# A hybrid attention block: the gate rows of the forgetting heads by broadcast loads from DRAM, and the head norm in three VectorE steps

## The chip, the cores and the metric

The kernel runs on one core of one Trainium2 chip. The metric is the device time of one execution in microseconds, where lower is better. A core has five engines with instruction streams of their own, which wait for each other by semaphores: TensorE (PE; the loading of its stationary operand is listed as PEld), VectorE (DVE), ScalarE (ACT), GpSimd (POOL) and SyncE (SP), which in this kernel issues nearly all DMA transfers. On-chip memory is SBUF (128 partitions) and PSUM, into which TensorE accumulates.

## The reference, cut to what matters

One layer with 512 positions (`T`), a width of 2048, eight stick-breaking heads ("sb"), eight forgetting heads ("fox") of 128 columns each, and a feed-forward part of 8192.

```python
def head_rmsnorm(o, g):
    of = o * lax.rsqrt(jnp.mean(o * o, axis=-1, keepdims=True) + EPS)
    ...
    return of * g

def forgetting_attention(q, k, v, log_f):
    c = lax.cumsum(log_f, axis=2)
    ...
        z = einsum('bhqd,bhkd->bhqk', qb, kb) * scale
        z = z + c[:, :, q0:end, None] - c[:, :, None, :end]
        p = softmax(where(causal, z, -inf), axis=-1)
        outs.append(einsum('bhqk,bhkd->bhqd', p, vb))

def reference(...):
    h = rmsnorm(x, g_attn)
    [qa, ka, va, qf, kf, vf, f] = split(h @ w_in)
    log_f = log_sigmoid(f + b_f)
    mixed = concat(head_rmsnorm(stick_breaking_attention(qa, ka, va), g_out_sb),
                   head_rmsnorm(forgetting_attention(qf, kf, vf, log_f), g_out_fox))
    x = x + mixed @ w_out
    x = x + relu(rmsnorm(x, g_mlp) @ w_up) ** 2 @ w_down
    return rmsnorm(x, g_final)
```

All inputs and the output are float32. For the change two things matter: in a forgetting head the row `-c[k]` is added to every row of the scores, and each head's output is divided by its root mean square over the 128 columns.

## The kernel before

**Arithmetic.** TensorE works on a 32-bit form (`fp32r`) of less than full precision, so every operand is split into a high and a low half: ScalarE casts the high half (`split`, L71 and L74), VectorE subtracts it to get the low half (L72, L75), and `mm3` (L104 to L106) makes one product of three matmuls. The products with W_out, W_up and W_down use seven products of half-size blocks in place of eight, which needs sums of weight blocks beforehand.

**Stages.** From the start to about 58 us x is transposed and normalised (`prepare`, `transpose_x`), while the first V projection and the eight gate columns f are accumulated over the 16 chunks of 128 rows (`accumulate_v`). Until about 640 us a loop `for n in range(0, 2 * NH, 2)` runs over pairs of heads, the forgetting heads 6, 7, 0 to 5 first and then the stick-breaking ones. For each head `project_q` makes q and k (two loads of `w_in` in `load_w`, L94, each followed by casts `wh` and subtractions `wl`, and 48 matmuls `accq`), and `attend_fox` or `attend_sb` computes the head. `sums_of_weights` prepares W_out beside that: it loads 2 MB of it into `mixed`, splits and subtracts, and stores `wraws`, `whigh` and `wsums` to DRAM scratch. Then come W_out, W_up and W_down, up to the end.

**Order.** In the attention part nobody writes the order out by hand. The tile framework runs a simulated timeline over the program and merges the heads' work (`attend` runs inside `tc.high_priority()`) with the projections; each engine then gets one fixed order. The order depends on which buffers are free. W_up and W_down follow an order of their own. SP's queue is one stream in that order too: an instruction on SP that waits for a semaphore holds up every transfer behind it.

**The gate row.** After the first V projection the gates' logarithms are summed along the positions by matmuls with a triangle of ones (`cps`), giving `cq`, with positions on the partitions and one column for each head. `cq` is split into a rounded part (`cr`) and the remainder, both copied into the zeroed tile `chl`, transposed by four matmuls (`cT`, L425) and cast into `ckT` (L427), with the two parts of each head in rows h and 8 + h. A selection matrix `nsel` is built at the start with GpSimd (L389, L391) and VectorE (L393): for each head it has -1 in the rows h and 8 + h, for all 128 columns. In `attend_fox` a matmul of `nsel` with `ckT` (L306) gives the negative gate row on all 128 partitions in PSUM, and ScalarE copies it to `cb` in SBUF (L308). VectorE then adds it to the scores together with the query's gate (`w`, L312), GpSimd masks (L243), and the softmax follows (L317 maximum, L318, L320 Exp, L321, L323).

**The head norm.** `weigh` (L246 to L286) transposes the probabilities (`pt`, L251), splits them, multiplies with V into `o`, squares `o`, and sums the squares over the 128 columns by two matmuls with ones into `q`, named `ssq` in the profile (L282, L283). VectorE makes `va = q / P + EPS` (L284), ScalarE makes Ln and Exp (L110, L111), so `ra` is a first value of 1/sqrt(va), and three VectorE steps (L112 to L114) improve it by one Newton step, `ra * (1.5 - 0.5 * va * ra * ra)`. The last step multiplies with the head's gain `gv` (L286) into `mixed`. For the last head (`left == 0`) the sums lie in a half of the score buffer.

**Buffers.** In the attention part PSUM has one buffer with the tag "o" (`cps`, `cT`, `ck`, `o` and `ssq` take turns in it) and one with the tag "s" (scores, `pt`). `cb` has one buffer (tag "ul5"). The weights have three buffers each (`wraw`, `wh`, `wl`).

Of the kernel before, what the change touches and what calls it, by code (L numbers as in the profile page):

```python
# [8 lines left out]
F32 = mybir.dt.float32  # L9
F32R = mybir.dt.float32r  # L10
# [4 lines left out]
P = 128  # L15
# [20 lines left out]
def block_kernel(ctx, tc, x, g_attn, w_in, b_f, g_out_sb, g_out_fox, w_out, g_mlp, w_up, w_down, g_final, y):  # L36
# [71 lines left out]
    def rsqrt(out, v, a, b):  # L108

        act.activation(a, v, AF.Ln)  # L110
        act.activation(a, a, AF.Exp, scale=-0.5)  # L111
        dve.scalar_tensor_tensor(b, a, -0.5, v, op0=ALU.mult, op1=ALU.mult)  # L112
        dve.tensor_tensor(b, b, a, op=ALU.mult)
        dve.scalar_tensor_tensor(out, b, 1.5, a, op0=ALU.add, op1=ALU.mult)  # L114
# [28 lines left out]
    g_rest = cp.tile([P, KC + 2 * NH], F32, name="g_rest")  # L143
    g_up, g_sb, g_fx = g_rest[:, :KC], g_rest[:, KC:KC + NH], g_rest[:, KC + NH:]
    bf = cp.tile([P, NH], F32, name="bf")
    cp.tile([P, 16], F32, name="pad1")
    sums = cp.tile([P, TB, 4], F32, name="ss1")
    ss1, last_sum, before_last = sums[:, :, :2], sums[:, 0, 2:3], sums[:, 1, 2:3]
    ss2 = cp.tile([P, TB, 4], F32, name="ss2")
# [2 lines left out]


    wsums = dp.tile([P, NH // 2, 4, 2, 2, NT], F32, name="wsums")
    whigh = dp.tile([P, NH // 2, 2, NT], F32, name="whigh")

    wraws = [dp.tile([P, NH // 2, 2, 2, NT], F32, name=f"wraws{p}") for p in (1, 2)]
# [8 lines left out]
    with tc.tile_pool(name="att", bufs=1, side="right", reuse_waits="tile") as at:  # L166
# [59 lines left out]
        def wide(name, dt=F32):  # L226
            return at.tile([P, 1280], dt, tag=name, name=name)
# [18 lines left out]
        def weigh(h, v, hc, w, gv, left=2):  # L246

            pt = atp.tile([P, 1536], F32, tag="s", name="pt")
            for j in range(TB):
                for i in range(j, TB):  # L250
                    last_heads[3] = pe.transpose(pt[:, OFF_T[j] + (i - j) * P:OFF_T[j] + (i - j + 1) * P],  # L251
                                 w[:, OFF_Q[i] + j * P:OFF_Q[i] + (j + 1) * P], ident)
            ph, pl = wide("ph", F32R), wide("pl", F32R)
            split(ph, pl, pt[:, :1280])
            hs = slice(hc * P, (hc + 1) * P)
            if left == 0:
                oq = atp.tile([P, 1536], F32, tag="s", name="oq")
                o, q = oq[:, :NT], oq[:, NT:2 * NT]
            else:
                o, q = atp.tile([P, NT], F32, tag="o", name="o"), None  # L260
            for j in range(TB):
                n = NT - j * P
                js = slice(OFF_T[j], OFF_T[j] + n)
                last_heads[0] = mm3(o[:, j * P:], v[0][:, j, hs], v[1][:, j, hs], ph[:, js], pl[:, js], j == 0, j == TB - 1)
            if left == 0:
                os_, ra = (at.tile([P, NT], F32, name=f"{c}_last") for c in ("os", "ra"))
            else:
                os_ = at.tile([P, NT], F32, tag="ul4", name="os")
                ra = at.tile([P, NT], F32, tag="uh5", name="ra")
            if left == 1:  # L270
                n1 = at.tile([P, 2 * NT], F32, tag="vh", name="n1", bufs=3)
                n2 = at.tile([P, 2 * NT], F32R, tag="vl", name="n2", bufs=3)
            else:
                n1, n2 = wide("ph"), wide("pl", F32R)
            sq, va = n1[:, :NT], n1[:, NT:2 * NT]
            sh, sl = n2[:, :NT], n2[:, NT:2 * NT]
            act.activation(sq, o, AF.Square)
            act.copy(os_, o)
            split(sh, sl, sq)
            if q is None:  # L280
                q = atp.tile([P, NT], F32, tag="o", name="ssq")
            pe.matmul(q, onesr, sh, start=True, stop=False)  # L282
            last_heads[1] = pe.matmul(q, onesr, sl, start=False, stop=True)  # L283
            dve.tensor_scalar(va, q, 1.0 / P, EPS, op0=ALU.mult, op1=ALU.add)  # L284
            rsqrt(va, va, ra, sq)
            dve.scalar_tensor_tensor(mixed[:, h, :], os_, gv, va, op0=ALU.mult, op1=ALU.mult)  # L286

        def attend_sb(h, v, hc, q, k):
# [13 lines left out]
            weigh(h, v, hc, w, g_sb[:, h:h + 1], NH - 1 - h)  # L302

        def attend_fox(h, v, hc, q, k):
            ck = atp.tile([P, NT], F32, tag="o", name="ck")
            pe.matmul(ck, nsel[:, h, :], ckT, start=True, stop=True)  # L306
            cb = at.tile([P, NT], F32, tag="ul5", name="cb")
            act.copy(cb, ck)  # L308
            s = scores(q, k)
            w = wide("w")  # L310
            for i, r in enumerate(rows(s)):
                dve.scalar_tensor_tensor(rows(w)[i], r, cq[:, i, h:h + 1], cb[:, :(i + 1) * P], op0=ALU.add, op1=ALU.add)  # L312
            causal(w, ALU.is_ge, NEG)
            ml = at.tile([P, P], F32, tag="ml", name="ml")
            mx, l = ml[:, :TB], ml[:, 16:16 + TB]
            for i, r in enumerate(rows(w)):
                dve.tensor_reduce(mx[:, i:i + 1], r, axis=mybir.AxisListType.X, op=ALU.max)  # L317
            dve.tensor_scalar(mx, mx, -1.0, None, op0=ALU.mult)  # L318
            for i, r in enumerate(rows(w)):
                act.activation(r, r, AF.Exp, bias=mx[:, i:i + 1], accum_out=l[:, i:i + 1])  # L320
            dve.reciprocal(l, l)  # L321
            for i, r in enumerate(rows(w)):
                dve.tensor_scalar(r, r, l[:, i:i + 1], None, op0=ALU.mult)  # L323
            weigh(NH + h, v, hc, w, g_fx[:, h:h + 1])
# [7 lines left out]
        with tc.tile_pool(name="tr0", bufs=2, space=PSUM) as trp:  # L332
# [35 lines left out]

            ps = accumulate_v([v_columns(order[0])], 2 * P + NH, [1, 1] + [2] * 7, prepare, trp)
            column_vectors(g_rest, *(g[0].rearrange("(h p) -> h p", p=P) for g in (g_mlp, g_out_sb, g_out_fox)))  # L370
            act.dma_start(bf, b_f.to_broadcast([P, NH]))
            r1 = row_rstd(ss1, "r1")
            psr = along_free(trp, r1, at.tile([P, NT], F32, tag="uh4", name="rw"))
# [10 lines left out]
            one = at.tile([P, P], F32, tag="ul5", name="one")  # L384
            pool.memset(one, 1.0)
            dve.tensor_copy(onesr, one)
            nsel = at.tile([P, NH, P], F32R, name="nsel")
            sel = wide("w")[:, :NH * P].rearrange("p (a b) -> p a b", a=NH)
            pool.memset(sel, 0.0)  # L389
            for shift in (0, NH):  # L390
                pool.affine_select(out=sel, in_=sel, compare_op=ALU.not_equal, fill=-1.0, base=-shift,  # L391
                                   pattern=[[-1, NH], [0, P]], channel_multiplier=1)
            dve.tensor_copy(nsel, sel)  # L393

        with tc.tile_pool(name="attp", bufs=1, space=PSUM, reuse_waits="tile") as atp:

            fl = at.tile([P, TB, NH], F32, name="fl")

            chl = at.tile([P, TB, P], F32, name="chl")
            pool.memset(chl, 0.0)  # L400
            cr = at.tile([P, TB, NH], F32R, name="cr")
            cq = at.tile([P, TB, NH], F32, name="cq")
            lf = at.tile([P, TB, 2 * NH], F32R, name="lf")
            fe = at.tile([P, TB, NH], F32, name="fe")
# [12 lines left out]
                              stop=(i == t), skip_group_check=True)  # L417
            act.copy(cq, cps[:, :, :NH])
            dve.tensor_tensor(cq, cq, cps[:, :, NH:], op=ALU.add)
            act.copy(cr, cq)  # L420
            dve.tensor_copy(chl[:, :, :NH], cr.bitcast(F32))
            dve.tensor_tensor(chl[:, :, NH:2 * NH], cq, cr.bitcast(F32), op=ALU.subtract)
            cT = atp.tile([P, NT], F32, tag="o", name="cT")
            for t in range(TB):
                pe.transpose(cT[:, t * P:(t + 1) * P], chl[:, t, :], ident)  # L425
            ckT = at.tile([P, NT], F32R, name="ckT")
            act.copy(ckT, cT)  # L427

            def sums_of_weights(m):

# [929 lines left out]
```

## Time and profile before

| | |
|---|---|
| device time, three runs | 2047.67, 2047.81, 2048.41 us; median 2047.81 |
| profiled execution, from its first to its last instruction | 2045.7 us |
| mean granted TensorE clock | 0.999 of full speed |
| VectorE instructions counted in the profile | 1892 |
| ScalarE instructions counted in the profile | 1578 |
| transfers of `w_in` issued by SP | 84 of 512 KB, 16 of 256 KB and a few smaller ones |

A row of a group of instructions reads: line, engine, operation, output and input tiles, their shape and type, the count; then busy us, mean ns of one; then the idle time of the engine just before them, and what ended most of it. A row of a timeline or of the chain that ended last begins with its start in us and its length. A row of the waits names who waited at which line, for whose result, how many us in total, how many times, and the longest. Busy times of matmuls overlap, so they don't add up. A releaser is inferred from semaphore events.

### The profile page before, as it was taken

Reading aid. Unit: us, or ns where it says so; the run is one execution under the profiler, and the core shown is the slowest. Engines: PE = TensorE matmul, PEld = TensorE weight load, DVE = VectorE, ACT = ScalarE, POOL = GpSimd, SP = SyncE. Lnnn points to the kernel's source line nnn. Section 1 sums busy time; section 2 is a strip of 40 time slices with the busy share of each in tenths; the row PEclk is TensorE's granted clock in tenths of the full one; section 3 lists DMA queues with packets and bytes.
Section 4 is the critical chain, followed back from the end, with each engine's and each line's share of the span. In section 5 each row is a group of like instructions: output and inputs, shape, how many; then the busy total and the mean of one; then the engine's idle time right before and its main releaser. Section 6 shows DMA issues by size and latency. Waiting matters only on the chain.

```text
span 2045.7 us, 26813 instructions
## 1 busy us (share of the span) xinstructions
PE 2030.4 (99%) x10322; PEld 1734.8 (85%) x10322; DVE 1666.6 (81%) x1892; ACT 1093.2 (53%) x1578; POOL 57.5 (3%) x76
## 2 busy tenths in 40 slices
PE   9999999999999999999999999999999999999998
PEld 8888888888888888988888888888888888888887
DVE  5667755566577678899999999999799898898896
ACT  6434433445455566677677676776644434444344
POOL 0000000000010000000000000000000000000004
PEclk9999999999999999999999999999999999999999
DMA  7888743232328882656666667667685674674642
GB/s 249 295 284 271 251 131 86 73 93 75 80 74 276 283 275 91 219 175 193 210 193 215 196 198 220 188 208 257 223 296 211 218 253 178 235 253 172 224 160 87
DMA packets 258848, 402.40 MB, mean 197 GB/s; under 512 B 9456, under 2 KB 154912, under 8 KB 251168
## 3 DMA queue, kind: packets, MB, share of 16 engines
q1 hardware_dynamic: 257760, 398.56, 59.4%
q10 hardware_dynamic: 960, 2.13, 0.3%
q8 instruction: 81, 1.33, 0.3%
q14 instruction: 47, 0.39, 0.1%
HBM read 307.85 MB, written 92.80 MB: 196 GB/s over the span
## 4 chain that ended last, share of the span: by engine, by line
PE 94%; DVE 4%; ACT 1%; issue 1%; DMA 1%; POOL 0%; SPq 0%; ACTq 0%; DVEq 0%
PE psa L594 10%; PE accd L104 8%; PE accd L105 8%; PE accd L106 8%; PE accq L104 6%; PE accq L105 6%; PE accq L106 6%; PE psa L596 5%; PE psc L594 5%; PE psc L596 3%; PE psb L594 3%; PE accv L104 2%; PE accv L105 2%; PE accv L106 2%; PE m L104 1%; PE m L105 1%
## 5 line engine op out<-in xcount | busy, mean ns | idle before, releaser
L1172 ACT CAST wh<-wd 128x1024 fp32r<-128x1024 f32 x126 | 124.9, 999 | 167.7 <-PE accd L106 54.4
L1062 DVE TENSOR_TENSOR wl<-wu,wh 128x1024 fp32r<-128x1024 f32 x157 | 191.4, 1220 | 15.3 <-ACT wh L1056 15.3
L104 PE MATMUL accq<-hH,wh 128*128 128x512 f32 x512 | 200.4, 391 | 0.4 <-DVE vl L75 0.4
L105 PE MATMUL accq<-hL,wh 128*128 128x512 f32 x512 | 200.2, 391 | 0.0
L106 PE MATMUL accq<-hH,wl 128*128 128x512 f32 x512 | 200.2, 391 | 0.0
L594 PE MATMUL psa<-f,wh 128*128 128x512 f32 x728 | 182.4, 392 | 0.3 <-ACT l L628 0.3
L1056 ACT CAST wh<-wu 128x1024 fp32r<-128x1024 f32 x157 | 166.2, 1058 | 28.5 <-issue 11.3
L105 PE MATMUL accd<-wl,uf 128*128 128x512 f32 x436 | 169.6, 389 | 0.0
L106 PE MATMUL accd<-wh,uf 128*128 128x512 f32 x436 | 169.6, 389 | 0.0
L104 PE MATMUL accd<-wh,uf 128*128 128x512 f32 x436 | 169.5, 389 | 0.0
L72 DVE TENSOR_TENSOR wl<-wraw,wh 128x1024 fp32r<-128x1024 f32 (+2 forms) x101 | 119.0, 1179 | 57.8 <-ACT wh L71 52.2
L71 ACT CAST wh<-wraw 128x1024 fp32r<-128x1024 f32 (+2 forms) x101 | 101.8, 1009 | 111.6 <-PE accq L105 68.6
L1179 DVE TENSOR_TENSOR wl<-wd,wh 128x1024 fp32r<-128x1024 f32 x126 | 143.9, 1151 | 13.2 <-ACT wh L1172 12.7
L594 PEld LDWEIGHTS psa<-f,wh 128*128 128x128 f32 x728 | 131.0, 189 | 24.0 <-ACT l L628 0.5
L946 DVE TENSOR_TENSOR m<-m,accd 128x1024 f32<-128x1024 f32 x84 | 102.2, 1216 | 46.7 <-PE accd L106 46.7
L1172 ACT CAST wx<-wd 128x1024 fp32r<-128x1024 f32 (+1 forms) x82 | 80.8, 995 | 109.3 <-PE accd L106 43.0
L104 PEld LDWEIGHTS accq<-hH,wh 128*128 128x128 f32 x512 | 96.1, 188 | 20.2 <-PE accv L106 0.8
L106 PEld LDWEIGHTS accq<-hH,wl 128*128 128x128 f32 x512 | 96.2, 188 | 19.3
L105 PEld LDWEIGHTS accq<-hL,wh 128*128 128x128 f32 x512 | 96.2, 188 | 19.3
L104 PE MATMUL accd<-wx,uf 128*128 128x512 f32 x284 | 110.5, 389 | 0.0
L105 PE MATMUL accd<-wx,uf 128*128 128x512 f32 x284 | 110.5, 389 | 0.0
L106 PE MATMUL accd<-wx,uf 128*128 128x512 f32 x284 | 110.5, 389 | 0.0
(375 smaller groups left out, 4930.1 us busy)
## 6 DMA issues: line engine op xcount, KB each, us to landing
wu<-in_w_up_dram SPq DMA_DIRECT2D x60, 1024.0 KB, 6.6
ufd<-st SPq DMA_DIRECT2D x98, 512.0 KB, 4.1
wd<-in_w_down_dram SPq DMA_DIRECT2D x48, 1024.0 KB, 7.6
wraw<-in_w_in_dram SPq DMA_DIRECT2D x84, 512.0 KB, 3.8
uf<-ufd SPq DMA_DIRECT2D x42, 1024.0 KB, 7.2
mixed<-in_w_out_dram SPq DMA_DIRECT2D x8, 2048.0 KB, 7.7
wsums<-mixed SPq DMA_DIRECT2D x8, 2048.0 KB, 7.3
wo<-wsums SPq DMA_DIRECT2D x28, 512.0 KB, 5.0
```

The lines of the kernel that those rows point to most:

```text
L71: ins = act.copy(hi, src)
L72: lows[0] = dve.tensor_tensor(lo, src, hi.bitcast(F32), op=ALU.subtract)
L104: pe.matmul(out, sh, mh, start=first, stop=False, skip_group_check=True)
L105: pe.matmul(out, sh, ml, start=False, stop=False, skip_group_check=True)
L106: return pe.matmul(out, sl, mh, start=False, stop=last, skip_group_check=True)
L594: pe.matmul(ps, hi[:, a, :], f_both(p, a), start=a == PAIRS[0] and p in (1, 5), stop=False, skip_group_check=True)
L596: ins = pe.matmul(ps[:, 2 * P:], lo[:, a, :], f_parts(p, a)[0], start=False, stop=a == PAIRS[-1], skip_group_check=True)
L946: dve.tensor_tensor(M[p][:, :, db, :], M[p][:, :, db, :], ps, op=ALU.add)
L1056: act.copy(rooms[k][0], srcs[k])
L1062: lows[0] = dve.tensor_tensor(lo, srcs.pop(k), hi.bitcast(F32), op=ALU.subtract)
L1172: act.copy(rooms[k + 3][0], srcs[k + 3])
L1179: dve.tensor_tensor(rooms[k + 2][1], srcs.pop(k + 2), rooms[k + 2][0].bitcast(F32), op=ALU.subtract)
```

## The change

The gate row no longer comes from a matmul. `cq` itself is transposed, into eight rows, which ScalarE multiplies by -1 into `ckT` (now [8, 512] in plain float32); SP stores that to a DRAM scratch `ckd`, and each forgetting head loads its row from there into `cb`, repeated on all 128 partitions, by one DMA on SP's queue. The selection matrix, `chl`, `cr`, the eight matmuls L306 and the eight copies L308 are gone.

In the head norm, Ln now reads the sums of squares from PSUM and does the scaling by 1/P and the addition of EPS itself, through the activation's scale and bias, the bias being a constant tile `eps`. The Newton step is done on `P * va` instead of `va`, in three VectorE steps: `(q + P * EPS) * ra`, times `ra`, and `(that - 3 * P) * ra`. Its result is -2P times the former one, and the gains of the heads are multiplied by -0.5/P once, after they are loaded. VectorE's step L284 is gone.

```diff
@@ -143,7 +143,9 @@
     g_rest = cp.tile([P, KC + 2 * NH], F32, name="g_rest")
     g_up, g_sb, g_fx = g_rest[:, :KC], g_rest[:, KC:KC + NH], g_rest[:, KC + NH:]
     bf = cp.tile([P, NH], F32, name="bf")
-    cp.tile([P, 16], F32, name="pad1")
+    eps = cp.tile([P, 1], F32, name="eps")
+    pool.memset(eps, EPS)
+    cp.tile([P, 8], F32, name="pad1")
     sums = cp.tile([P, TB, 4], F32, name="ss1")
     ss1, last_sum, before_last = sums[:, :, :2], sums[:, 0, 2:3], sums[:, 1, 2:3]
     ss2 = cp.tile([P, TB, 4], F32, name="ss2")
@@ -152,6 +154,7 @@
 
 
     wsums = dp.tile([P, NH // 2, 4, 2, 2, NT], F32, name="wsums")
+    ckd = dp.tile([NH, NT], F32, name="ckd")
     whigh = dp.tile([P, NH // 2, 2, NT], F32, name="whigh")
 
     wraws = [dp.tile([P, NH // 2, 2, 2, NT], F32, name=f"wraws{p}") for p in (1, 2)]
@@ -281,8 +284,11 @@
                 q = atp.tile([P, NT], F32, tag="o", name="ssq")
             pe.matmul(q, onesr, sh, start=True, stop=False)
             last_heads[1] = pe.matmul(q, onesr, sl, start=False, stop=True)
-            dve.tensor_scalar(va, q, 1.0 / P, EPS, op0=ALU.mult, op1=ALU.add)
-            rsqrt(va, va, ra, sq)
+            act.activation(ra, q, AF.Ln, scale=1.0 / P, bias=eps)
+            act.activation(ra, ra, AF.Exp, scale=-0.5)
+            dve.scalar_tensor_tensor(sq, q, P * EPS, ra, op0=ALU.add, op1=ALU.mult)
+            dve.tensor_tensor(sq, sq, ra, op=ALU.mult)
+            dve.scalar_tensor_tensor(va, sq, -3.0 * P, ra, op0=ALU.add, op1=ALU.mult)
             dve.scalar_tensor_tensor(mixed[:, h, :], os_, gv, va, op0=ALU.mult, op1=ALU.mult)
 
         def attend_sb(h, v, hc, q, k):
@@ -302,10 +308,8 @@
             weigh(h, v, hc, w, g_sb[:, h:h + 1], NH - 1 - h)
 
         def attend_fox(h, v, hc, q, k):
-            ck = atp.tile([P, NT], F32, tag="o", name="ck")
-            pe.matmul(ck, nsel[:, h, :], ckT, start=True, stop=True)
             cb = at.tile([P, NT], F32, tag="ul5", name="cb")
-            act.copy(cb, ck)
+            sp.dma_start(cb, ckd[h:h + 1, :].to_broadcast([P, NT]))
             s = scores(q, k)
             w = wide("w")
             for i, r in enumerate(rows(s)):
@@ -368,6 +372,7 @@
 
             ps = accumulate_v([v_columns(order[0])], 2 * P + NH, [1, 1] + [2] * 7, prepare, trp)
             column_vectors(g_rest, *(g[0].rearrange("(h p) -> h p", p=P) for g in (g_mlp, g_out_sb, g_out_fox)))
+            dve.tensor_scalar(g_rest[:, KC:], g_rest[:, KC:], -0.5 / P, None, op0=ALU.mult)
             act.dma_start(bf, b_f.to_broadcast([P, NH]))
             r1 = row_rstd(ss1, "r1")
             psr = along_free(trp, r1, at.tile([P, NT], F32, tag="uh4", name="rw"))
@@ -384,21 +389,11 @@
             one = at.tile([P, P], F32, tag="ul5", name="one")
             pool.memset(one, 1.0)
             dve.tensor_copy(onesr, one)
-            nsel = at.tile([P, NH, P], F32R, name="nsel")
-            sel = wide("w")[:, :NH * P].rearrange("p (a b) -> p a b", a=NH)
-            pool.memset(sel, 0.0)
-            for shift in (0, NH):
-                pool.affine_select(out=sel, in_=sel, compare_op=ALU.not_equal, fill=-1.0, base=-shift,
-                                   pattern=[[-1, NH], [0, P]], channel_multiplier=1)
-            dve.tensor_copy(nsel, sel)
 
         with tc.tile_pool(name="attp", bufs=1, space=PSUM, reuse_waits="tile") as atp:
 
             fl = at.tile([P, TB, NH], F32, name="fl")
 
-            chl = at.tile([P, TB, P], F32, name="chl")
-            pool.memset(chl, 0.0)
-            cr = at.tile([P, TB, NH], F32R, name="cr")
             cq = at.tile([P, TB, NH], F32, name="cq")
             lf = at.tile([P, TB, 2 * NH], F32R, name="lf")
             fe = at.tile([P, TB, NH], F32, name="fe")
@@ -417,14 +412,12 @@
                               stop=(i == t), skip_group_check=True)
             act.copy(cq, cps[:, :, :NH])
             dve.tensor_tensor(cq, cq, cps[:, :, NH:], op=ALU.add)
-            act.copy(cr, cq)
-            dve.tensor_copy(chl[:, :, :NH], cr.bitcast(F32))
-            dve.tensor_tensor(chl[:, :, NH:2 * NH], cq, cr.bitcast(F32), op=ALU.subtract)
             cT = atp.tile([P, NT], F32, tag="o", name="cT")
             for t in range(TB):
-                pe.transpose(cT[:, t * P:(t + 1) * P], chl[:, t, :], ident)
-            ckT = at.tile([P, NT], F32R, name="ckT")
-            act.copy(ckT, cT)
+                pe.transpose(cT[:NH, t * P:(t + 1) * P], cq[:, t, :], ident)
+            ckT = at.tile([NH, NT], F32, tag="ul4", name="ckT")
+            act.mul(ckT, cT[:NH, :], -1.0)
+            sp.dma_start(ckd, ckT)
 
             def sums_of_weights(m):
 
```

Counted in the two programs: TensorE has 8 instructions fewer, VectorE 18 fewer (16 in the norms, the cast of `nsel`, and two for `chl`, with one added for the gains), ScalarE 9 fewer, GpSimd 3 fewer, and SP 9 transfers more: one store of 16 KB and eight loads that write 256 KB each.

The scheduler's order changes as well. On TensorE the first 388 matmuls and the last 6958 keep their order; everything that moves lies between about 40 and 690 us. There the forgetting heads stand earlier among the projections than before, since the matmul L306 no longer takes a turn in the PSUM buffer "o". On SP the first load of `cb` follows the store of `ckd` with one store of `wraws` between them; the second to the fourth stand among the stores of `sums_of_weights` and the loads of `w_in`, the sixth and the seventh shortly behind a 2 MB load of W_out, and the eighth among the loads of `w_in`. From the second on each waits until VectorE has read `cb` of the head before (L312).

## The prediction

> **What bounds the kernel now.** I read the page's head and its engine line first, then the shares of the chain that ended last, then every wait of TensorE.
>
> ```profile
> span 2045.7 us, 26813 instructions
> PE 2030.4 (99%) x10322; PEld 1734.8 (85%) x10322; DVE 1666.6 (81%) x1892; ACT 1093.2 (53%) x1578; POOL 57.5 (3%) x76
> PE 94%; DVE 4%; ACT 1%; issue 1%; DMA 1%; POOL 0%; SPq 0%; ACTq 0%; DVEq 0%
> ...
> PE trg L335 <- POOL chl L400: 3.3, 1, 3.3
> PE tr L179 <- DVE wl L72: 1.0, 1, 1.0
> PE psa L106 <- DVE wl L72: 1.0, 1, 1.0
> PE oq L104 <- DVE pl L72: 0.5, 1, 0.5
> PE accq L104 <- DVE vl L75: 0.4, 1, 0.4
> PE accoa L104 <- ACT g L71: 0.4, 1, 0.4
> PE psa L594 <- ACT l L628: 0.3, 1, 0.3
> ```
>
> TensorE is the bound: it is busy for 99% of the span and has 94% of the chain. Its waits (total, times, longest) are seven in the whole run, 6.9 us together. The first two belong to the start, the third and the last to the stage of W_up; the change leaves their work as it is. What it can win by waits is the middle three, 0.5 + 0.4 + 0.4 = 1.3 us. VectorE, at 81%, has room. So a change helps here by the matmuls that it takes out, and hurts as far as TensorE waits for something new.
>
> The span is 2045.7 us and the median of the runs is 2047.81, so 2.1 us lie around the span. I put the sum on the span and add the same 2.1.
>
> **The matmuls.** What one costs is the spacing of the starts, not its busy time of 0.39, since they overlap:
>
> ```profile
> 75.39 0.39 PE L104 MATMUL accq<-hH,wh 128*128 128x512 f32 x1
> 75.62 0.39 PE L306 MATMUL ck<-ckT,nsel 128*128 128x512 f32 x1
> 75.84 0.39 PE L105 MATMUL accq<-hL,wh 128*128 128x512 f32 x1
> ...
> L306 PE MATMUL ck<-ckT,nsel 128*128 128x512 f32 x8 | 3.1, 389 | 0.0
> L308 ACT COPY cb<-ck 128x512 f32<-128x512 f32 x8 | 4.7, 586 | 10.0 <-PE ck L306 10.0
> L284 DVE TENSOR_SCALAR ph<-ssq 128x512 f32<-128x512 f32 x14 | 9.6, 682 | 8.1 <-PE ssq L283 8.1
> L112 DVE SCALAR_TENSOR_TENSOR ph<-ra,ph 128x512 f32<-128x512 f32 x14 | 9.6, 686 | 2.9 <-ACT ra L111 2.7
> ```
>
> The selection matmul takes its slot of (75.84 - 75.39) / 2 = 0.225 us like its neighbours. There are eight (x8 in the L306 row), none behind a gap: 8 x 0.225 = **-1.8 us**. The four cT transposes stay four.
>
> [...]
>
> **The copies on ScalarE and the norm's step.** Eight copies of 0.586 us (L308) and sixteen steps of 0.68 us (L284: these 14 and two of the last heads) go, 4.7 us on ScalarE and 10.9 us on VectorE. Both lie under TensorE's work: VectorE's idle time before L284 ended by ssq, not the other way round, and no row of TensorE's waits names a norm but the one at 650.8, below. I cost them at **0**. If the cover were gone and VectorE set the pace, the 10.9 us would be won; that is a rival. The new first step (q + c) * ra is of the form of L112, 0.686, and reads PSUM; the square-sum buffer is now held through Ln, Exp and that step, some 2 us instead of 0.68, and the next o in it comes a head later. The setup (nsel, chl, cr) lies beside the first projection: 0. The scaling of 16 gain columns is one short step: 0.
>
> **The wait at 338.60** (accq <- vl) is the end of a chain that begins with a row of ck:
>
> ```profile
> 331.65 0.24 PE ck L306
> 331.89 0.02 issue
> 331.91 0.60 ACT cb L308
> ...
> 337.67 0.80 DVE vl L75 x2
> 338.47 0.14 issue
> 338.60 0.47 PE accq L104
> ```
>
> The matmul and copy are gone, and in the changed program's order the forgetting heads' scores come earlier (without ck in the PSUM buffer "o" the scheduler moves the heads), so w and ml no longer sit ahead of these two vl: **-0.4 us**. Bounds: -0.4 and 0 (the same meeting elsewhere).
>
> **The gate row by DMA.** Each cb is now 256 KB through SP's queue, eight of them, and one store of 16 KB ahead. The nearest rows:
>
> ```profile
> wraw<-in_w_in_dram SPq DMA_DIRECT2D x84, 512.0 KB, 3.8
> whigh<-thi SPq DMA_DIRECT2D x8, 256.0 KB, 2.2
> bf<-in_b_f_dram ACTq DMA_DIRECT2D x1, 4.0 KB, 4.9
> ...
> 72.90 0.58 ACT L427 CAST ckT<-cT 128x512 fp32r<-128x512 f32 x1
> ...
> 77.41 0.68 DVE L72 TENSOR_TENSOR tboth<-mixed,tboth 128x512 fp32r<-128x512 f32 x1
> 80.88 1.92 DVE L312 SCALAR_TENSOR_TENSOR w<-s,cq,cb 128x128 f32<-128x128 f32 x4
> 89.73 1.27 DVE L323 TENSOR_SCALAR w<-w,ml 128x128 f32<-128x128 f32 x4
> 92.40 0.38 PE L251 MATMUL pt<-ident,w 128*128 128x128 f32 x2
> ```
>
> For the first head: ckT is done at 72.90 + 0.58 = 73.5; a store takes 2.2 us by the whigh row and the load back between 2.2 (whigh's size) and 4.9 (bf's broadcast), so cb stands at 77.9 to 80.6. In the new order VectorE's w comes right behind tboth, at about 78.1 (77.41 + 0.68), ahead of qf, a mixed step and a wl that now run in front of it. VectorE would stand for 0 to 2.5 us; I take about 1, the load being nearer to a plain one of its size. Its cover: w itself is 80.88 - 78.1 = 2.8 us earlier than before, and the transposes at 92.40 come 1.4 us after L323's end (89.73 + 1.27 = 91.0). Queued behind w on VectorE is the wl of w_in, used some 27 matmuls later, about 6 us. So **0**, between 0 and +1; without that cover each further microsecond would be one of TensorE's.
>
> [...]
>
> The other seven loads wait on SP until the head before has read cb (one buffer) and, in the order, are used 23 us of TensorE work or more after their issue, against landings of at most 4.9: **0**. What can go wrong is what stands behind them on SP: the loads of w_in.
>
> ```profile
> SPq L94 <- DVE wl L72: 346.4, 77, 10.8
> L71 ACT CAST wh<-wraw 128x1024 fp32r<-128x1024 f32 (+2 forms) x101 | 101.8, 1009 | 111.6 <-PE accq L105 68.6 <-PE accv L106 26.1 <-issue 9.7
> ```
>
> Those already wait for VectorE, 346.4 / 77 = 4.5 us each, so a cb whose wait ends sooner costs nothing. Their first reader, the cast wh, sat idle for TensorE to free its buffers (68.6, 26.1) and not for the DMA: the loads are early. In both orders at least 8.3 us of TensorE work stand between a load and its cast, 4.5 more than its median of 3.8: **0**, up to what the rival A makes of it.
>
> **The last head.** Here the order is shorter by some 1.5 us of TensorE work between the last scores and their transposes, a cast g of a 1024-column form comes between two steps of ScalarE (1.01 us, the mean of the wh row) and one vl (0.80 / 2 = 0.4) on VectorE.
>
> ```profile
> 627.66 0.77 POOL L243 TENSOR_SCALAR_AFFINE_SELECT w<-w 128x384 f32<-128x384 f32 x2 [6.03 <-ACT w L300]
> 630.00 1.12 PEld L251 LDWEIGHTS pt<-ident,w 128*128 128x128 f32 x10
> 643.46 0.70 DVE n L284
> ...
> 650.36 0.41 ACT g L71
> 650.82 0.50 PE accoa L104
> ```
>
> The masked w was ready at 628.43 and its transposes began loading at 630.00, a slack of 1.6. Used up by 1.5 + 1.0 + 0.4 = 2.9, that makes a new wait of **+1.3 us**, between 0 (the cast slips in unseen) and 2.9. The wait at 650.8 follows from the chain of both last norms, which has two steps of 0.68 less: more than its 0.4, so **-0.4**, at worst 0. The 0.5 of oq <- pl stays.
>
> **Sum:** -1.8 - 0.4 + 0 + 0 + 1.3 - 0.4 = -1.3 on the span: 2044.4, and with 2.1 around it **2046.5 us**.
>
> **The rivals.**
>
> A, slower: **SP's queue holds back weights.** A cb load is put where the w of the head before should just be done. If VectorE runs late there, SP stands at it and all w_in, w_out and scratch transfers behind it stand too. It decides from a hold of 4.5 us, the margin above. If SP has to wait for as long as VectorE's softmax of one head runs (80.88 to 91.0, 10.1 us), 5.6 us are lost on TensorE: one such place gives 2046.5 + 5.6 = 2052.1, two 2057.7. For it: SP waits on VectorE already, up to 10.8 us once, and behind each of the eight loads stand loads of w_in. Against it: wh's idle row, which names no DMA.
>
> B, **no change:** the removed matmuls lie in slack and the small waits move: 2047.8. The spacing of 0.225 speaks against it.
>
> C, more: **all three small waits go** and the last head's doesn't come: -1.8 - 1.3 = -3.1, 2044.7. The order around the last head speaks against it.
>
> D, **VectorE sets the pace** in attention: 10.9 us of its steps and 1.8 of TensorE are won, 2035.1. TensorE's seven waits, three of them in attention, are nearly proof against it.
>
> **How the numbers follow.** What tells no change from a change here is about 0.2%, 4.1 us: 2043.7 to 2051.9. Forecast 0.58 (own range 2044.7 to 2049.9: C's end, and every term at its dear end, -1.8 + 0 + 1 + 2.9 + 0 = +2.1 on 2047.8), A 0.27, B 0.07, C 0.05, D 0.03. Faster by more than that: D and the far tail of C, some waits of the start going too, 0.06. Slower: A, 0.27. Same: the rest, 0.67. For eight in ten the range takes the forecast, B, C and more than half of A: 2043.5 to 2056.
>
> **What would show it.** Right: 10314 matmuls; TensorE's waits without accq <- vl, with one of about 1.3 us at the pt of the last head; VectorE's wait for cb once, near 78 us, under 2.5; w_out's stage 1.3 us earlier. SP's rows of waits with cb: if they are over 4.5 us each and wh's idle time names wraw's DMA, A is right. Wrong in kind: waits of TensorE in the heads in between, or starts at other than 0.227 apart.

## The result and the profile after

The changed kernel takes 2051.38 us (median of 14 runs, 2050.27 to 2052.91), the kernel before 2047.32 us beside it (14 runs, 2046.30 to 2048.41): a ratio of 1.0019, 95% interval 1.0013 to 1.0026. That is 4.1 us slower, where 1.3 us faster was forecast. The time lies in the range, but on the other side of no change.

The page's head and engine line, and all waits of TensorE (line, releaser, total us, times, longest) of the changed kernel:

```profile
span 2049.2 us, 26770 instructions
PE 2029.7 (99%) x10314; PEld 1736.0 (85%) x10314; DVE 1655.0 (81%) x1874; ACT 1089.9 (53%) x1569; POOL 54.3 (3%) x73
...
PE pt L254 <- POOL w L246: 5.0, 1, 5.0
PE trg L339 <- DMA g_rows<-in_g_attn_dram: 3.3, 1, 3.3
PE psa L106 <- DVE wl L72: 1.0, 1, 1.0
PE tr L182 <- DMA mixed<-in_x_dram: 1.0, 1, 1.0
PE psa L587 <- ACT l L621: 0.3, 1, 0.3
```

The eight matmuls are gone (10314), and so are all three small waits of the attention part. In their place stands one wait of 5.0 us: the last head's transposes `pt` for GpSimd's mask (`w`, L246). The windows around it show a second loss (length, busy us of TensorE, weight loads, VectorE, ScalarE and GpSimd with their counts, then the granted clock, DMA share, GB/s):

```profile
625.00:630.00 5.00, 3.21 (x18) 2.68 (x16) 5.00 (x9) 3.03 (x5) 1.22 (x1) 1.00 0.92 330
630.00:635.00 5.00, 1.83 (x9) 1.84 (x10) 2.49 (x4) 0.20 (x1) 3.11 (x2) 0.62 0.18 73
635.00:640.00 5.00, 5.00 (x18) 4.08 (x17) 3.15 (x4) 3.00 (x4) 0.00 (x0) 0.70 0.01 3
640.00:645.00 5.00, 5.00 (x27) 4.31 (x27) 4.21 (x8) 2.92 (x5) 0.00 (x0) 1.00 0.60 210
```

Behind the pause the granted clock is 0.62 and 0.70, means over these windows, and from 640 on it is 1.00 again. The timelines of the three engines at that place (start, length):

```profile
627.28 0.47 DVE L75 SCALAR_TENSOR_TENSOR vl<-accv,r1v,vh 128x256 fp32r<-128x256 f32 x1
627.67 2.15 DVE L72 TENSOR_TENSOR g<-mixed,g 128x1024 fp32r<-128x1024 f32 x3
629.74 2.15 DVE L523 TENSOR_TENSOR mixed<-mixed 128x1024 f32<-128x1024 f32 x3
631.81 0.68 DVE L72 TENSOR_TENSOR n<-n,n 128x512 fp32r<-128x512 f32 x1
...
628.78 4.33 POOL L246 TENSOR_SCALAR_AFFINE_SELECT w<-w 128x384 f32<-128x384 f32 x2 [6.42 <-ACT w L306]
...
633.16 2.40 PE L254 MATMUL pt<-ident,w 128*128 128x128 f32 x10 [4.96 <-POOL w L246]
635.21 0.78 PE L104 MATMUL accoa<-wx,g 128*128 128x512 f32 x1
635.78 0.63 PE L105 MATMUL accoa<-wx,g 128*128 128x512 f32 x1
636.21 0.63 PE L106 MATMUL accoa<-wx,g 128*128 128x512 f32 x1
636.64 0.63 PE L104 MATMUL accoa<-wx,g 128*128 128x512 f32 x1
```

The same place in the kernel before, where the mask had run from 627.66 to 628.43: the start of VectorE's train `g`, the transposes, and the window around them.

```profile
629.42 2.15 DVE L72 TENSOR_TENSOR g<-mixed,g 128x1024 fp32r<-128x1024 f32 x3
630.10 1.25 PE L251 MATMUL pt<-ident,w 128*128 128x128 f32 x10
...
630.00:635.00 5.00, 4.57 (x29) 3.71 (x27) 5.00 (x7) 2.74 (x4) 0.00 (x0) 1.00 0.66 224
```

The two mask instructions, 0.77 us together before, take 4.33, from 628.78 to 633.11. Around that time VectorE runs seven instructions without a gap, all with both operands in SBUF (`g`, `mixed`, `n`; called the train from here on), from 627.67 to 632.49, and the mask ends behind them. Then the transposes need 2.40 us instead of the 1.25 of before, and matmuls of 512 columns start 0.43 us apart (636.21 to 636.64) instead of 0.227.

The change's gain was there until then. Setting the starts of the same matmuls (counted from the end) of the two profiled executions side by side, the changed kernel is 0.5 us ahead at 66 us, where only the arrival of x differs, 2.5 us ahead at 623 us, and 2.8 us behind from 694 us on. So attention brought 2.0 us, and the 70 us around the last head cost 5.3. (The two spans, with what stands around the matmuls, differ by 3.5 us, and the medians by 4.1.)

Other rows answer to steps of the prediction: SP's wait at the loads of `cb`, the cast `wh`, and VectorE's first step with `cb`, with the DMA's time to landing.

```profile
SPq L312 <- DVE ml L321: 21.8, 5, 6.8
...
L71 ACT CAST wh<-wraw 128x1024 fp32r<-128x1024 f32 (+2 forms) x101 | 101.9, 1010 | 147.2 <-PE accq L105 78.1 <-PE accv L106 60.5 <-DMA wraw<-in_w_in_dram 4.2
...
77.69 1.93 DVE L316 SCALAR_TENSOR_TENSOR w<-s,cq,cb 128x128 f32<-128x128 f32 x4 [0.57 <-DMA cb<-ckd]
...
cb<-ckd SPq DMA_DIRECT2D x8, 256.0 KB, 3.5
```

### The profile page after: what moved, and what is told of

It is laid out like the page before. It is cut to its first block, busy times and chain, and to the rows that moved or that the text cites. A ratio compares the mean times of both kernels' runs of the same rounds, so it can differ in the third digit from the quotient of the medians.

```text
span 2049.2 us, 26770 instructions
## 1 busy us (share of the span) xinstructions
PE 2029.7 (99%) x10314; PEld 1736.0 (85%) x10314; DVE 1655.0 (81%) x1874; ACT 1089.9 (53%) x1569; POOL 54.3 (3%) x73
## 4 chain that ended last, share of the span: by engine, by line
PE 65%; DVE 2%; ACT 1%; issue 0%; DMA 0%; ACTq 0%
PE psa L587 10%; PE accd L105 8%; PE accd L106 8%; PE accd L104 8%; PE psa L589 5%; PE psc L587 5%; PE psc L589 3%; PE psb L587 3%; PE m L104 1%; PE m L105 1%; PE m L106 1%; PE psb L589 1%; PE accoa L104 1%; PE accoa L105 1%; PE accoa L106 1%; PE accob L104 1%
```

## The experiments

Times are medians beside the kernel before on the same chip; that kernel itself lies between 2047.3 and 2048.8 us from one set of runs to the next, so the ratios compare, not the times. The masks and rows on scratch tiles have no ratio, since their work is added to the kernel.

| run | us | before | ratio, 95% interval |
|---|---|---|---|
| norm_only | 2052.50 | 2048.49 | 1.0019, 1.0009 to 1.0028 |
| gate_only | 2047.52 | 2048.49 | 0.9997, 0.9988 to 1.0006 |
| probe | 2048.23 | 2048.49 | 1.0000, 0.9991 to 1.0009 |
| fill | 2053.88 | 2048.49 | 1.0029, 1.0018 to 1.0041 |
| hold_pl | 2045.92 | 2048.82 | 0.9987, 0.9978 to 0.9996 |
| hold_exp | 2049.63 | 2048.82 | 1.0005, 0.9996 to 1.0014 |
| norm_hold | 2046.89 | 2048.82 | 0.9995, 0.9985 to 1.0004 |
| pause_2 | 2048.79 | 2048.24 | 1.0001, 0.9993 to 1.0010 |
| pause_5 | 2055.31 | 2048.24 | 1.0036, 1.0022 to 1.0049 |

### Which half of the change loses the time

`norm_only` is the kernel before with the norm's lines of the diff; `gate_only` is the changed kernel without them.

```diff
 norm_only, against before
-            dve.tensor_scalar(va, q, 1.0 / P, EPS, op0=ALU.mult, op1=ALU.add)
-            rsqrt(va, va, ra, sq)
+            act.activation(ra, q, AF.Ln, scale=1.0 / P, bias=eps)
...
+            dve.scalar_tensor_tensor(va, sq, -3.0 * P, ra, op0=ALU.add, op1=ALU.mult)
 gate_only, against before
-            pe.matmul(ck, nsel[:, h, :], ckT, start=True, stop=True)
-            act.copy(cb, ck)
+            sp.dma_start(cb, ckd[h:h + 1, :].to_broadcast([P, NT]))
```

> The kernel before with the head norm's part of the change alone: Ln from PSUM, three VectorE steps, gains scaled once; the selection matmuls and copies stay. Theory T (the loss is the last head's mask on GpSimd, held up by a train of VectorE instructions that read two SBUF operands, and the slower TensorE clock after the pause; the train's place came with the norm's edit): the order at the last head is that of the changed kernel here too, so the mask takes some 4.3 us in place of 0.77, TensorE waits some 5 us at pt, runs at about half clock for some 5 us behind it, and the kernel is slower than before by 5.0 + 2.3 - 1.3 (waits that go) = 5 to 7 us. Rival G (the loss is the gate rows' DMA in SP's queue): no loss, 0 to -1 us.

> The changed kernel with the head norm of the kernel before: the gate rows come by DMA, the eight matmuls and copies are gone, the norm keeps its four VectorE steps. Theory T: the last head's order is that of the kernel before, the mask takes 0.77 us, no wait over 1.5 us at pt, clock 1.00, and the kernel is faster than before by the matmuls and the small waits, 1.5 to 3 us. Rival G: slower than before by about the 4 us of the whole change.

The norm's part alone has the ratio of the whole change, 1.0019. Its masks and its wait:

```profile
PE pt L253 <- POOL w L245: 5.0, 1, 5.0
...
630.66 4.33 POOL L245 TENSOR_SCALAR_AFFINE_SELECT w<-w 128x384 f32<-128x384 f32 x2 [6.42 <-ACT w L305]
```

The gate rows alone cannot be told from no change. The last head's mask takes 0.77 us there and nobody waits for it, but the expected gain of 1.5 to 3 us did not come. Two other waits stand in its profile.

```profile
PE ssq L284 <- DVE pl L72: 2.2, 2, 1.9
...
PE ssq L283 <- ACT pl L71: 0.7, 1, 0.7
...
110.00:115.00 5.00, 3.05 (x14) 2.15 (x13) 5.00 (x10) 1.57 (x2) 1.73 (x2) 0.98 0.76 255
115.00:120.00 5.00, 5.00 (x17) 3.99 (x16) 4.37 (x8) 2.37 (x9) 0.00 (x0) 0.68 0.21 36
```

An early head's sums of squares wait for VectorE, which is busy without a gap from 110 to 115 us, and the clock falls behind that pause too, to 0.68. By the starts of its matmuls the profiled execution loses 3.9 us there. That execution took 2050.99 us, the longest of the 11, whose median is 2047.52, so most of the others lose less; no trace shows where. So the DMA is not what costs the changed kernel its time. The changed kernel has neither of these waits. Whether it is the norm's saved step that removes them was not tried by itself.

### Does the wait end when VectorE lets the mask go first?

`probe` lets VectorE's train start only after the mask, by a copy of one column of the masked tile; `hold_pl` puts the train behind the last head's `pl` as well. `norm_hold` has the latter with the norm's part alone.

```diff
 probe
             causal(w, ALU.is_gt, 0.0)
+            if h == NH - 1:
+                masked[0] = dve.tensor_copy(spare[:, :1], w[:, 896:897])
...
+                    with tc.issue_after(masked[0].ins):
+                        lows[0] = dve.tensor_tensor(lo, src, hi.bitcast(F32), op=ALU.subtract)
...
+                with tc.issue_after(masked[0].ins):
+                    g_form(5, (4, 8), (0, 2), (2, 3))
 hold_pl, norm_hold: the copy, and
             split(ph, pl, pt[:, :1280])
+            masked[1] = lows[0]
...
             with tc.issue_after(last_heads[2].ins):
+                pass
+            with tc.issue_after(masked[1].ins):
                 for p in (4, 5):
                     g_form(p, (4, 8), (0, 2), (2, 3))
```

> The changed kernel with one VectorE copy of 128x1 that reads the last head's masked w, put ahead of the train g, mixed, so that the train starts after the mask. Theory T: the mask takes 0.77 us, TensorE's wait at pt falls from 5.0 to about 1.4 us, the clock stays at 1.00 between 625 and 645 us; the train now delays pl, so oq waits about 2 us; against the changed kernel -3.6 - 2.3 + 2.0 = about -4 us. Rival R (GpSimd's long span is only a matter of the record, and pt waits for something else): the wait at pt stays near 5 us or grows, no gain.

> The changed kernel with the 128x1 copy that reads the last head's masked w, and the whole train g, mixed behind the last head's pl, not only behind the mask. Theory T: the mask takes 0.77 us, TensorE waits 1.4 us at pt and at most 0.5 us at oq, and no 3 us of pause come together, so the clock stays near 1.00; 5 to 6 us faster than the changed kernel, 1 to 2 us faster than before. Rival R (pt waits for something else): no better than the run in which the train only followed the mask.

> The norm's part of the change alone with the train g, mixed behind the last head's pl. Theory T (the norm's edit costs time only by the train's place): the 4 us that it lost alone are gone, and it stands within 1 us of the kernel before. Rival N (the norm's own steps cost time, on all sixteen heads): still 2 us or more slower than before.

TensorE's waits at the last head in `probe`, then `hold_pl`'s with its mask and its windows:

```profile
PE oq L104 <- DVE pl L72: 1.8, 1, 1.8
PE pt L254 <- POOL w L246: 1.4, 1, 1.4
```

```profile
PE pt L254 <- POOL w L246: 1.4, 1, 1.4
...
629.27 0.76 POOL L246 TENSOR_SCALAR_AFFINE_SELECT w<-w 128x384 f32<-128x384 f32 x2 [6.42 <-ACT w L307]
...
630.00:635.00 5.00, 4.92 (x27) 4.23 (x28) 3.15 (x4) 2.23 (x4) 0.03 (x1) 1.00 0.34 131
635.00:640.00 5.00, 5.00 (x27) 4.34 (x26) 5.00 (x9) 4.36 (x8) 0.00 (x0) 1.00 0.62 210
```

In `probe` both waits are the expected ones, 1.4 and 1.8 us, but the clock fell to 0.72 between 635 and 640 us all the same, so it gained a little less than the 4 us. In `hold_pl` only the 1.4 us are left and the clock stays at 1.00; it is faster than both kernels (0.9987 of the one before, with an interval of 0.9978 to 0.9996). By the starts of its matmuls it is 2.0 us ahead at 623 us, and 2.5 us at its last matmul. `norm_hold` no longer shows the norm's loss and cannot be told from no change, so the 4 us did not come from the sixteen norms themselves.

`hold_exp` also moves the casts of the train behind the last Exp on ScalarE, to take the remaining 1.4 us.

```diff
-            act.activation(w, w, AF.Exp)
+            masked[2] = act.activation(w, w, AF.Exp)
...
+            for p in (4, 5):
+                with tc.issue_after(masked[1].ins), tc.issue_after(masked[2].ins):
                     g_form(p, (4, 8), (0, 2), (2, 3))
```

> The same, and the casts g that belong to the train are put behind the last head's second Exp on ScalarE, so the 1.05 us cast between Exp and Ln goes too. Theory T: TensorE's wait at pt falls from 1.4 to about 0.3 us; some 1 us faster than the run before this one in the list, 2 to 3 us faster than the kernel before. Rival R2 (another step sets the last head's pace): the wait at pt stays at 1.4 us.

```profile
PE ssq L286 <- ACT n L71: 2.8, 1, 2.8
...
PE pt L254 <- POOL w L246: 0.7, 1, 0.7
```

The wait at `pt` did fall, to 0.7, but the moved casts stand ahead of the other head's `n` on ScalarE, and its sums of squares wait 2.8 us. It lost what `hold_pl` had won.

### Is the slow clock a consequence of the pause?

`fill` puts work that nobody reads into the pause; `pause_2` and `pause_5` lengthen it in `hold_pl` by doing the mask again, without any help of VectorE's.

```diff
 fill
             pt = atp.tile([P, 1536], F32, tag="s", name="pt")
+            if left == 0:
+                for _ in range(30):
+                    pe.matmul(pt[:, 1280:], hH[0][:, :P], hH[0][:, :2 * P], start=True, stop=True, skip_group_check=True)
 pause_2 (and 5 in place of 2)
             if h == NH - 1:
+                for _ in range(2):
+                    causal(w, ALU.is_gt, 0.0)
```

> The changed kernel with 30 matmuls of 256 columns, whose result nobody reads, in the unused columns of the transposes' buffer ahead of the last head's pt: 30 x 0.12 = 3.6 us of TensorE work in the pause. Theory T: the mask still takes over 4 us, but TensorE stands for only 1 to 1.5 us, the granted clock stays at 1.00 and the transposes take 1.2 us in place of 2.4: some 2.3 us faster than the changed kernel, less what the scheduler shifts. Rival C (the low clock has nothing to do with the pause): the clock between 630 and 640 us stays near 0.65 and the time where it was.

> The kernel with the train behind pl, with the last head's mask done three times over (it changes nothing the second time): GpSimd works 1.6 us longer ahead of the transposes, without VectorE in its way. Theory T (a pause of TensorE costs itself, and from some length on also a stretch of slow clock): the wait at pt becomes 1.4 + 1.6 = 3.0 us, and the time grows by 1.6 us without a slow stretch or by up to 4 us with one. Rival C (the clock's fall has another cause): 1.6 us, clock 1.00.

> The same with the mask six times over: 4.1 us longer. Theory T: a wait at pt of 5.5 us, the granted clock behind it falls to 0.6 to 0.75 over some 5 to 10 us, matmuls of 512 columns start 0.43 us apart for a while, and the time grows by 4.1 + 2.3 = about 6.4 us. Rival C: by 4.1 us alone, clock 1.00, matmuls 0.23 us apart right behind the pause.

`fill` settles nothing: the scheduler moved other work with the added matmuls, TensorE waited 1.0 us for a `vl` ahead of them and ran them at a clock of 0.77, and the kernel became slower. The longer pauses do show it. Their windows, `pause_2` first:

```profile
630.00:635.00 5.00, 3.45 (x13) 3.04 (x14) 1.23 (x2) 1.25 (x3) 2.00 (x5) 0.68 0.33 133
635.00:640.00 5.00, 5.00 (x26) 4.25 (x26) 4.25 (x6) 2.27 (x4) 0.00 (x0) 0.98 0.20 47
```

```profile
630.00:635.00 5.00, 3.07 (x10) 2.05 (x11) 2.69 (x5) 1.32 (x2) 3.39 (x9) 0.51 0.17 66
635.00:640.00 5.00, 5.00 (x21) 4.21 (x21) 4.10 (x5) 1.53 (x2) 0.00 (x0) 0.80 0.00 0
```

The clock falls to 0.68 and 0.51, against 1.00 in the same kernel without the added masks. The waits at `pt` of 3.0 and 5.5 us that were expected did not come as such, since the new order puts matmuls of the other head's `ssq` into the pause: TensorE waits 2.0 us for `n` and 0.8 for the mask in `pause_2`, and 2.0, 0.4 and 1.5 us in `pause_5`. Against `hold_pl`, by the ratios, `pause_2` costs (1.0001 - 0.9987) x 2048 = 2.9 us for 1.6 us of masks, within what T allowed; `pause_5` costs 10 us instead of 6.4, and by the starts of its matmuls 4.4 of them are lost at a new wait of W_up that came with its order (psa for `f`, 3.6 us).

### What holds the mask up

The same two masks as at the last head, on a scratch tile ahead of the first projection, beside rows of VectorE instructions. `port`'s rows were broken up by other instructions; `port_2` to `port_5` differ in what stands ahead of the row and in its operands. The core of `port_5`:

```diff
+                for stall in (1, 1, 1, 0, 0, 0):
...
+                    held[1] = act.activation(wt, one_, AF.Copy)
+                    causal(wt, ALU.is_gt, 0.0)
+                    for i in range(6):
+                        with tc.issue_after(prev.ins):
+                            prev = dve.tensor_tensor(two_[1 + i % 3], one_[:, :NT], one_[:, NT:2 * NT], op=ALU.add)
```

> The changed kernel with four masks on GpSimd on a scratch tile of ones ahead of the first projection, each started by a small VectorE copy: the first with nothing behind it on VectorE, the second beside six VectorE additions of 128x512 with both operands in SBUF, the third beside six with one operand in PSUM, the fourth beside six maximum reductions of 128x1024 in SBUF. Theory T: the 384-column mask takes 0.52 us beside nothing, reductions and PSUM additions, and as long as the row of additions lasts, some 3 to 4 us, in the second case. Rival B (any busy VectorE slows GpSimd in proportion): the second to the fourth take about the same.

> The scratch masks ahead of the first projection once more, with four VectorE instructions of 128x512 standing in one row behind each starting copy: none, additions of two SBUF operands, additions with one operand in PSUM (one other instruction comes between them), maximum reductions in SBUF. Theory T: the mask of 384 columns takes 0.52 us in the first, third and fourth case, and in the second as long as the row lasts, 4 x 0.6 + 0.4 = about 2.8 us. Rival S (only the one addition that is already running holds the mask up): 0.9 to 1.1 us in the second.

> Scratch masks again, now as at the last head: the mask is released by a ScalarE step of 1.3 us over the whole tile, which starts together with a row of eight VectorE additions of 128x512 that wait for nothing; so the mask comes when the row has been running for more than 1 us. Four cases: no row; both operands in SBUF; one operand in PSUM; both in SBUF, read in four blocks of 128 columns with gaps between. Theory T2 (a mask that comes when a row of two-operand SBUF instructions is already under way waits for the row's end): 0.5 us, some 4 us, 0.5 us, some 4 us. Rival S (it waits only for the instruction that is running, as in the earlier scratch run): 0.5, 0.6 to 1.1, 0.5, 0.6 to 1.1 us, and the next addition is the longer by it.

> Scratch masks beside rows of eight VectorE additions of 128x512 from SBUF as in the run before, six rows: whole operands, both operands in blocks with gaps, the first operand alone in blocks (as in g), and the three again with the mask released 0.13 us sooner. Theory P (what lets the mask in between two additions is that the operands are whole; blocks with gaps keep it out to the row's end): 0.6 to 1.1 us in the first and fourth row, 3 to 4 us in the others, whatever the moment of release. Rival M (the moment of arrival within the running addition decides): the first and fourth differ from each other, or rows with blocks are short at one of the moments.

> Scratch masks beside rows of six VectorE additions of 128x512 from whole SBUF operands, all rows alike, the mask released 1.3 us after the row's start. Ahead of the first three rows VectorE stands and waits for ScalarE; ahead of the last three it comes without a wait from four maximum reductions. Theory Q (a row whose first instruction had to wait lets the mask in after the running addition; a row that VectorE reached without a wait keeps it out to the end): 0.7 to 1.0 us in the first three, 2.5 to 3 us in the last three. Rival A (it goes by turns: one mask is let in, the next kept out): the six rows alternate.

In `port` and `port_2` the mask of 384 columns took 0.91 us beside additions of two SBUF operands, and 0.52 beside nothing, beside additions with an operand in PSUM and beside reductions; in `port_2` the addition behind it took 1.00 instead of 0.68. It was let in after the addition already running, as S had it, and not at the row's end. The two masks of each row (x2) in `port_3` (no row; whole operands; PSUM; blocks with gaps), `port_4` and `port_5`:

```profile
5.62 0.77 POOL L247 TENSOR_SCALAR_AFFINE_SELECT w<-w 128x384 f32<-128x384 f32 x2 [4.25 <-ACT w L385]
7.77 1.45 POOL L247 TENSOR_SCALAR_AFFINE_SELECT w<-w 128x384 f32<-128x384 f32 x2 [1.38 <-ACT w L385]
13.05 0.77 POOL L247 TENSOR_SCALAR_AFFINE_SELECT w<-w 128x384 f32<-128x384 f32 x2 [3.84 <-ACT w L385]
17.90 4.01 POOL L247 TENSOR_SCALAR_AFFINE_SELECT w<-w 128x384 f32<-128x384 f32 x2 [4.08 <-ACT w L385]
```

```profile
5.62 1.53 POOL L247 TENSOR_SCALAR_AFFINE_SELECT w<-w 128x384 f32<-128x384 f32 x2 [4.25 <-ACT w L385]
11.01 4.00 POOL L247 TENSOR_SCALAR_AFFINE_SELECT w<-w 128x384 f32<-128x384 f32 x2 [3.85 <-ACT w L385]
16.38 1.45 POOL L247 TENSOR_SCALAR_AFFINE_SELECT w<-w 128x384 f32<-128x384 f32 x2 [1.37 <-ACT w L385]
21.54 4.14 POOL L247 TENSOR_SCALAR_AFFINE_SELECT w<-w 128x384 f32<-128x384 f32 x2 [3.71 <-ACT w L385]
26.93 1.58 POOL L247 TENSOR_SCALAR_AFFINE_SELECT w<-w 128x384 f32<-128x384 f32 x2 [1.24 <-ACT w L385]
32.22 4.15 POOL L247 TENSOR_SCALAR_AFFINE_SELECT w<-w 128x384 f32<-128x384 f32 x2 [3.71 <-ACT w L385]
```

```profile
6.97 1.50 POOL L247 TENSOR_SCALAR_AFFINE_SELECT w<-w 128x384 f32<-128x384 f32 x2 [5.61 <-ACT w L396]
12.12 1.44 POOL L247 TENSOR_SCALAR_AFFINE_SELECT w<-w 128x384 f32<-128x384 f32 x2 [3.64 <-ACT w L396]
...
23.71 2.80 POOL L247 TENSOR_SCALAR_AFFINE_SELECT w<-w 128x384 f32<-128x384 f32 x2 [5.07 <-ACT w L396]
29.82 2.80 POOL L247 TENSOR_SCALAR_AFFINE_SELECT w<-w 128x384 f32<-128x384 f32 x2 [3.31 <-ACT w L396]
...
```

`port_3` has both outcomes, 1.45 and 4.01, and neither T2 nor S holds for both. In `port_4` short and long rows alternate whatever their operands (whole ones in the first and the fourth), so P falls. M falls by the moments themselves: the masks of the second and third row start 0.31 and 0.30 us into an addition, those of the fourth and fifth 0.17 and 0.18, and each pair has a long and a short one. `port_5` tells apart what remains: with a wait of VectorE ahead of the row the masks take 1.44 to 1.50 us three times, without one 2.80 (2.81 once) three times, which is to the row's end. That fits Q, and not plain alternation. In the short rows of `port_2` and `port_3`, and in the third and fifth of `port_4`, VectorE had waited for the mask before just ahead of the row (0.41 to 1.90 us). One row speaks against Q as a full rule: the first of `port_4` is short, 1.53 us, though its trace shows no wait of VectorE ahead of it.

At the last head of the changed kernel the train follows `vl` at 627.67 without a gap, and VectorE is busy from 625 to 632.5: a row without a wait ahead of it. The mask, ready at 628.78, came after the first of its seven instructions had started and was kept out until the last.

## Why the prediction was wrong, and where it was right

**The last head, the step that failed.** The prediction gave it +1.3 us, at most 2.9, as a wait of `pt` for the masked `w`. The direction and the reason (less TensorE work, a cast and a `vl` more ahead of the transposes) were right, and so was the size as far as it went: with the mask at its old length the wait is 1.4 us in `probe` and `hold_pl`. What failed is that the mask's 0.77 us were taken over from before. In the new order VectorE's train of two-operand SBUF instructions starts 1.1 us ahead of the mask (627.67 against 628.78) and the mask takes 4.33; before, the train began behind the mask. That is 3.6 of the 5.0 us. The slowdown behind it was not in the sum at all: the transposes take some 0.9 us longer between their starts, the first `accoa` 0.35 and five others 5 x 0.2, 2.3 us together. 5.0 + 2.3 in place of 1.3 is 6.0 us more, less 0.5 for oq (below), which takes the forecast of -1.3 to +4.2, where +4.1 was measured. The agreement is closer than the account: by the starts of the matmuls the stretch lost 5.3 us, and not 5.0 + 2.3 - 0.5 - 0.4 = 6.4, so some 1 us came back in W_out's first part, and the medians lie 0.6 us further apart than the profiled spans. Neither is explained here.

**The norm's step at 0.** As a saving on VectorE it was rightly costed at about nothing: `norm_hold`, 0.9985 to 1.0004, cannot be told from no change. But the edit moved the order at the last head, and `norm_only` lost 4 us by that. The prediction looked for the reordering among the gate rows; it was the hidden step, costed at 0, that brought it.

**The matmuls and the waits.** -1.8 - 0.4 were forecast for attention before the last head; the starts show 2.0. The wait at 650.8 is gone as forecast, and the 0.5 of oq <- pl went too.

**The gate row at 0.** VectorE stood 0.57 us for the first `cb` (0 to 2.5 forecast, about 1 taken), the loads took 3.0 to 4.5 us to land, and no wait of TensorE names them.

**Rival A,** with the largest chance of the losing side, did not happen. SP waited 21.8 / 5 = 4.4 us at loads of `cb`, just under the 4.5 from which it was to decide, though 6.8 us once, and the DMA is the least of the three that the row of `wh` names (4.2 us in all). No wait of TensorE in attention is left but the one at `pt`. The time came out on A's side for another reason, so it is luck that the range, drawn up to 2056 for A's sake, holds it. B, C and D did not happen either.

## What to carry to other kernels

When an edit lets a scheduler reorder, take no duration over from the old trace for a GpSimd instruction on the critical path before looking at what VectorE runs beside it in the new order: here 0.77 us became 4.33. A step that is rightly worth nothing can still move its neighbours, so try each half of a change alone. And a pause of TensorE can cost more than itself: behind the pauses of 1.9 us (`gate_only`) and 1.8 us (`probe`) came 3.41 us at half the clock, so a new pause of that size should be priced with and without such a stretch, some 1.7 us by these figures, an estimate.

## What the runs showed of the hardware that was not expected

**VectorE and GpSimd.** A GpSimd mask in SBUF that arrives in a row of VectorE additions with both operands in SBUF was let in after the running addition in all seven rows ahead of which VectorE had waited: in `port_2` the mask of 384 columns took 0.91 us, and the next addition 1.00 instead of 0.68; in the other six rows the two masks together took 1.44 to 1.58 us (`port_3` to `port_5`; 0.77 beside nothing). It was kept out to the row's end in seven of the eight rows where VectorE had not waited: the two masks took 2.80 to 2.81 us beside six additions (`port_5`) and 4.00 to 4.15 beside eight (`port_3`, `port_4`); in the eighth (`port_4`) 1.53. Beside additions with an operand in PSUM and beside reductions the mask of 384 columns took 0.52, as beside nothing (`port`, `port_2`). At the last head of the changed kernel it stayed out for a train of seven instructions, and the two masks took 4.33 us. Why a wait ahead of the row matters, and whether it is the wait or the pause that comes with it, is not shown.

**The clock.** One pause of 1.9 us was enough for a granted clock of 0.68 over the 5 us behind it (`gate_only`, 113.9 us), and one of 1.8 us for 0.72 (`probe`, some 6 us behind another of 1.4), while 1.4 us alone (`hold_pl`) and 2.8 us (`hold_exp`) left it at 1.00. Windows with other bounds suggest why a longer pause can do less. The granted clock has only two values there, 1.00 and 0.50: in the changed kernel it is 0.50 from 631.20 to 638.03. Amid the work it stays at 0.50 for 3.41 us (`norm_only`, `gate_only`, `probe`, `fill`, `pause_2`) or for twice that, 6.83 us (the changed kernel, `pause_5`). The changed kernel's next change, at the end of its work, comes at 2044.32 us, 1406.29 us behind the one at 638.03, which is 412 times 3.4133. Counted off in steps of 3.41 us from such an edge, the step before a fall had TensorE busy for 0.42 us in the changed kernel, 1.46 in `gate_only`, 1.61 in `probe` and 1.77 in `fill`; the emptiest step at the pause of `hold_pl` had 2.02 and no fall behind it. The pause of `hold_exp` lies across an edge, so its two steps were busy for 2.43 and 1.59 us and the clock stayed. So the share of one step that a pause takes fits these runs better than its length; between about 1.6 and 1.8 us busy both outcomes stand, so the limit is not sharp here, and no run shows what makes the steps. The expectation of `hold_pl` reckoned with 3 us of pause, about what the two waits of `probe` make together (1.4 + 1.8 = 3.2); by the steps the fall in `probe` follows the 1.8 alone. Each kernel has one trace, and its other executions need not have had their steps at the same place: the mean granted clock of `hold_exp` lies between 0.997 and 0.999 from run to run.
